# Hybrid decoder step on one core: pieces of the weights placed by the feature rows that they meet, units on feature rows eight apart, cache rows copied in pieces

## The chip, the cores and the metric

The kernel runs on one core of a Trainium2 chip. The metric is the device time of one execution in microseconds; of several runs the median counts. A profiled execution of the kernel gives a page of summaries and a trace that can be asked for single instructions.

## The reference, cut to what matters

One layer of a decoder works on 256 prompt rows and 8 sample rows, which share all weights. `IN_DIM` is 13856 columns, `D_FF` is 5632.

```python
h = RMSNorm(x)
q, k, v, z, xbc, dt, qm, g = split(h @ w_in)            # 2048 x 13856
a = sliding_window_attention(q, k, v)                    # sample: over a cache of 128 rows
s = ssd(xbc, z, dt)                                      # chunked scan, 32 heads
m = cross_attention(qm, mem)                             # mem @ w_mem_kv (2048 x 2048) for the prompt
x = x + (sig(gA)*(a @ w_up_swa) + sig(gB)*(s @ w_up_ssd) + sig(gM)*(m @ w_up_mem)) @ w_out
x = x + (silu(h2 @ w_gate) * (h2 @ w_up)) @ w_down       # h2 = RMSNorm(x), 2048 x 5632 and back
# also returned: the new keys, values, states, and the sample caches moved on by one row
```

Everything is float32. The sample caches `s_swa_k`, `s_swa_v` hold 127 old rows and one new one per sample, so 127 rows of 1 KB are copied for each of 8 samples, for keys and for values.

## The kernel before, in words

**Features and weights.** Activations lie in SBUF with the feature on the partition: feature row k is a slice of 128 partitions x 264 columns (256 prompt, 8 sample) of float32. Eight rows make one tile of `half` (pool `ap`, ten buffers); `Feat` is two such tiles, 16 rows of 2048 features. A weight matrix is used in groups of 512 output columns. A group has 4 PSUM tiles (128 output features each) and goes through its input features in units of two rows k. One unit is one load of 2 x 128 x 512 weights (512 KB) into `raw`.

**The split.** To keep precision, each unit's weights are split (`do_split`, helper `split`, L181 and L182): ScalarE writes `hi`, rounded to float32r, and VectorE writes `lo`, the rest. Features are split in the same way (`hh`/`hl`, `h2h`/`h2l`, `fah`/`fal`, `aTh`/`aTl`, `mTh`/`mTl`, `sT`, `mg`). A product is then three matmuls: hi with the high features, hi with the low ones, lo with the high ones. So a unit is 4 pieces c x 2 rows k x 3 = 24 matmuls of 128x128 weights with 264 moving columns. The helper `mm` records all of them at L160; they are told apart by the PSUM tile's name: `pin` (input projection), `pus`, `pum`, `pua` (the three up projections), `pout`, `pg`, `pu` (gate and up of the feed-forward), `pdn` (down). The memory projection `pmem` is turned round: there the features (`memh`, `meml`, 128 columns) are loaded as weights and 512 columns of `hi` or `lo` move.

**Addresses.** A feature row is 264 x 4 = 1056 bytes a partition, which is 4 x 256 + 32: each next row begins 32 bytes further within 256, and after eight rows it comes round. A piece of weights is 128 x 4 = 512 bytes, a whole multiple of 256. In the built program all `hi` and `lo` buffers begin at 128 within 256, so every piece does. With *offset* the text means the start of a piece minus the start of the feature row that moves with it, within 256 bytes. Before, it takes the eight values 0, 32, ..., 224, depending on the row alone. (The tile of `h2h` begins at 192 within 256, that of `hh` at 64: for `h2h` row 12 has offset 64 and row 13 has 32.)

**Order of the work.** A list `units` holds all units. The loop at the end of the kernel walks it: `feed` loads four units ahead and splits three ahead, then the unit's matmuls follow, then `after` of a group (which reads the PSUM tiles), then a slice of the side work (`side`, `slow`: attention, SSD, norms), whose pieces are told by estimated microseconds. A scheduler then places the recorded instructions, so that two units can be mixed in some places. Weight loads are issued on SP's queue, most other transfers on POOL's. `behind_split(d)` makes a DMA wait for the split last issued. `move_rows` copies the cache rows from DRAM to DRAM, in two DMAs of 1 MB and a small one for the convolution, and is called when the last group of `pout` begins.

```python
for k in range(2):
    kk = 2 * u + k
    wh = hi[:, k * 512 + c * P:k * 512 + (c + 1) * P]
    wl = lo[:, k * 512 + c * P:k * 512 + (c + 1) * P]
```

Of the kernel before, what the change touches and what calls it, by code (L numbers as in the profile page):

```python
# [18 lines left out]
P = 128  # L19
D = 2048  # L20
NP = 256
# [56 lines left out]
def tile_hybrid_decoder_step(  # L78
# [198 lines left out]
    def do_split(n):  # L277
        if n < state["split"]:
            return
        raw = raws.pop(n)  # L280
        hi = wp.tile([P, 1024], F32R, tag="hi", name=nm("hi"), bufs=3)
        lo = wp.tile([P, 1024], F32R, tag="lo", name=nm("lo"), bufs=3)
        if units[n].get("whole"):
            act(hi.bitcast(F32)[:, 0:512], raw[:, 0:512], AF.Copy)
        elif units[n].get("perm"):
            for k in range(2):
                v = [t[:, k * 512:(k + 1) * 512].rearrange("p (r a d) -> p a r d", r=4, a=2) for t in (hi, lo)]
                s = raw[:, k * 512:(k + 1) * 512].rearrange("p (a r d) -> p a r d", a=2, r=4)
                state["split_at"], state["rest_at"] = split(v[0], v[1], s)
        else:  # L290
            for k in range(2 if n == 0 else 1):
                c = slice(512 * k, 512 * k + 512) if n == 0 else slice(0, 1024)
                with tc.issue_after(state["memh", k if n == 0 else 1].ins):
                    state["split_at"], state["rest_at"] = split(hi[:, c], lo[:, c], raw[:, c])
        parts[n] = (hi, lo)
        state["split"] = n + 1

    def std_loads(src):
# [3 lines left out]

    def group(name, loads, nk, xh, xl, after, perm=False, before=None, middle=None):

        st = {}

        def prod(u):
            def f(hi, lo):
                if u == 0:
                    if before:  # L310
                        before()
                    st["ps"] = [dps(name)[:, 0:NT] for _ in range(4)]
                if middle and 2 * u == nk // 2:
                    middle()
                for c in range(4):
                    for k in range(2):
                        kk = 2 * u + k
                        wh = hi[:, k * 512 + c * P:k * 512 + (c + 1) * P]
                        wl = lo[:, k * 512 + c * P:k * 512 + (c + 1) * P]
                        mm(st["ps"][c], wh, xh(kk), start=kk == 0, stop=False)  # L320
                        mm(st["ps"][c], wh, xl(kk), start=False, stop=False)
                        mm(st["ps"][c], wl, xh(kk), start=False, stop=kk == nk - 1)
            return f

        for u in range(nk // 2):
            units.append(dict(
                loads=loads(u), perm=perm, prod=prod(u),
                after=(lambda: after(st["ps"])) if u == nk // 2 - 1 else None))

    def w_loads(w, col):  # L330
        return lambda u: std_loads(w[2 * u * P:(2 * u + 2) * P, col:col + 512])

# [37 lines left out]
    def mem_group(cg):  # L370
        st = {}

        def prod(u):
            def f(hi, lo):
                if u == 0:
                    st["ps"] = [dps("pmem") for _ in range(2)]
                for n, (t, k) in enumerate(((0, 0), (1, 0), (0, 1), (1, 1))):
                    if cg == 0 and n == 1 and u < 7:

                        with tc.issue_after(m.ins):  # L380
                            mem_feats(u + 1)
                    kk = 2 * u + k
                    mh = memh(kk)[:, t * P:(t + 1) * P]
                    ml = meml(kk)[:, t * P:(t + 1) * P]
                    wh, wl = hi[:, k * 512:(k + 1) * 512], lo[:, k * 512:(k + 1) * 512]
# [51 lines left out]
        for u in range(KT // 2):  # L437
            units.append(dict(
                loads=loads(u), 
                prod=prod(u), after=(after_k if cg < 2 else after_v) if u == KT // 2 - 1 else None))  # L440
# [74 lines left out]
    nd = const([P, 256], "nd")  # L515
    slope = const([P, 16], "slope")
    nslope = const([P, 16], "nslope")
    islope = const([P, 16], "islope")
    sink = const([P, 16], "sink")
    nsink = const([P, 16], "nsink")  # L520
    cols = const([P, 4], "cols")
    slope_c, islope_c, sink_c = cols[:, 0:1], cols[:, 1:2], cols[:, 2:3]
    blk2 = const([P, 62], "blk2")
    jm = const([32, 16], "jm")
    kn_bc = const([P, 64], "kn_bc")
    dtb_bc = const([P, 32], "dtb_bc")
# [70 lines left out]

    def move_rows():

        for dst, src in ((s_swa_k, cache_swa_k), (s_swa_v, cache_swa_v)):  # L600
            to, of = (t[0].rearrange("b t h d -> b (t h d)")[:, o:o + 127 * 256].rearrange("b (s e) -> s b e", s=16)
                      for t, o in ((dst, 0), (src, 256)))
            tc.keep_in_program_order(nc.gpsimd.dma_start(to, of))
        nc.gpsimd.dma_start(s_conv[0, :, 0:2], state_conv[0, :, 1:3])


# [225 lines left out]

    kT = const([P, 2, NT], "kT")

    v_new = const([P, 2, NS], "v_new")

# [260 lines left out]
    dt_tok = const([P, 64], "dt_tok")  # L1097
    last = const([P, 11, 24], "last")
    acs_tok = const([P, 64], "acs_tok")
# [8 lines left out]
    def conv(ct, raw, dst):  # L1108
# [10 lines left out]
        V.tensor_tensor(acc[:, :, NP:NT], acc[:, :, NP:NT], pre[:, ct:ct + 4], op=ALU.add)  # L1119
        act(dst, acc, AF.Silu)  # L1120
        V.tensor_copy(last[:, :, ct:ct + 4].rearrange("p r c -> p c r"), raw[:, :, NP - 3:NT])
        if ct == 12:
# [21 lines left out]

    def task_b():
        ssd["B"] = const([P, 4, NT], "BT")
        yield from conv(16, ssd["Braw"], ssd["B"])
# [40 lines left out]
    def task_dt():  # L1188
        ssd["dsc"] = const([P, 16, 17], "dsc", tag="nd")
        s3 = const([P, 3, 16, NS], "s3", tag="kT")  # L1190
        ssd["xsS"], ssd["zsS"], ssd["ysS"] = (s3[:, i] for i in range(3))
# [159 lines left out]
    def ssd_norm_work(g):  # L1351
        ssd[f"s{g}"] = half("sT", F32R)
        y, z = ssd[f"y{g}"][:, :, 0:NP], ssd[f"z{g}"]
# [27 lines left out]
        yield None  # L1381
        hi, lo = ssd[f"s{g}"][:, 0:4, 0:NP], ssd[f"s{g}"][:, 4:8, 0:NP]
        act(hi, y, AF.Copy)
# [25 lines left out]
    def ssd_sample_end():  # L1409
# [18 lines left out]
        for g in range(4):  # L1428
            split(ssd[f"s{g}"][:, 0:4, NP:NT], ssd[f"s{g}"][:, 4:8, NP:NT], t[:, 4 * g:4 * g + 4])
        yield 3  # L1430
# [107 lines left out]
    def up_mem(i):  # L1538
        branch("pum", C_G + 4096 + 512 * i, w_loads(w_up_mem[0], 512 * i),
               lambda k: mT["h"][:, k], lambda k: mT["l"][:, k].bitcast(F32R), mg_d[:, i],  # L1540
               middle=split_m if i == 0 else None)
# [42 lines left out]
    def after_ups(i):  # L1584
        def f(ps):
            mg[i] = half("mg", F32R)
            for c in range(4):
                tm = t1("mgs")
                V.tensor_tensor(tm, ps[c], mg["s", i][:, c], op=ALU.mult)
                V.tensor_tensor(tm, tm, mg["w", i][:, c], op=ALU.add)  # L1590
                split(mg[i][:, c], mg[i][:, 4 + c], tm)
        return f

    for i in range(4):
        group("pus", w_loads(w_up_ssd[0], 512 * i), KT, lambda k: ssd[f"s{k // 4}"][:, k % 4],
              lambda k: ssd[f"s{k // 4}"][:, 4 + k % 4], after_ups(i), before=lambda i=i: before_ups(i),
              middle=lambda i=i: middle_ups(i))

# [8 lines left out]
    def after_out(i):  # L1607
        def f(ps):
            if i == 0:
                x2["x"] = Feat("x2", F32)  # L1610
                x2["h"], x2["l"] = Feat("h2h"), Feat("h2l")
                x2["s"] = const([P, NT], "sqsum", tag="kT")
            for c in range(4):
# [22 lines left out]
    def before_out(i):  # L1636
        load_x(i)
        if i == 3:
            move_rows()

    for i in range(4):
        group("pout", w_loads(w_out[0], 512 * i), KT, lambda k: mg[k // 4][:, k % 4], lambda k: mg[k // 4][:, 4 + k % 4], after_out(i),
              before=lambda i=i: before_out(i))
# [28 lines left out]
    def down(i, base, nt_, last):  # L1672
# [32 lines left out]

        def loads(u):
            r = (4 * base + 2 * u) * P
            return std_loads(w_down[0, r:r + 2 * P, 512 * i:512 * (i + 1)])

        group("pdn", loads, nt_, lambda k: ffn["h"](k), lambda k: ffn["l"](k), after)  # L1710

    for base, ng in ((0, 4), (4, 4), (8, 3)):
# [33 lines left out]
    for i, u in enumerate(units):  # L1746
# [52 lines left out]
```

## Time and profile before

| what | value |
|---|---|
| median of 3 runs | 1902.41 us (1901.97 to 1904.27) |
| span of the profiled execution, first to last instruction | 1901.3 us |
| time of that execution beside its span | not listed apart; the runs shown lie 0.7 to 3.0 us above the span |
| TensorE busy | 1893.6 us, 100% of the span |
| VectorE, ScalarE, GpSimd busy | 1176.5, 959.8, 114.9 us |
| bytes moved | 402.08 MB, mean 211 GB/s |

Matmuls are pipelined: a row of the trace gives a matmul's start and a duration of some 285 ns, while the next one starts some 120 ns later. So the cost of a matmul is read from the distance between starts, or from the time of a whole stretch divided by its count, never from the mean duration. Rows of the timeline are rounded to 10 ns; a distance between two single rows is good to 10 ns, one over nine rows to about 1 ns each.

### The profile page before, as it was taken

The page shows a single profiled execution, that of the slowest core. Times are in us where ns is not written, and L with a number is a line of the kernel's source. Part 1 is how long each engine was busy: PE and PEld are TensorE (multiplying, and loading weights), DVE is VectorE, ACT ScalarE, POOL GpSimd, SP SyncE. Part 2 cuts the span into 40 slices and gives each one's busy share as a digit, 9 for nine tenths or more (in the row PEclk, how much of TensorE's full clock was granted, in tenths as well). Part 3 has the DMA queues.
Part 4 walks back from the last instruction along what each step waited for, and adds up shares of the span by engine and source line. Part 5 has one row for each costly group of instructions (what it writes and reads, how often), then busy time and mean ns, then how long its engine had stood idle before and what let it go on. Part 6 is the DMA issues. An engine that isn't in the chain of part 4 may idle for free.

```text
span 1901.3 us, 37640 instructions
## 1 busy us (share of the span) xinstructions
PE 1893.6 (100%) x15359; PEld 1848.2 (97%) x15359; DVE 1176.5 (62%) x2263; ACT 959.8 (50%) x1403; POOL 114.9 (6%) x237
## 2 busy tenths in 40 slices
PE   9999999999999999999999999999999999999999
PEld 7899999989999999999999999999999999999999
DVE  5755578666787868787455665555445555445554
ACT  6654466655767676764443444444334444334443
POOL 1110001011011111110000000000000000000000
PEclk9999999999999999999999999999999999999999
DMA  8776679678777777797768556665566665566654
GB/s 303 234 235 201 203 229 298 199 226 256 215 220 250 238 243 234 234 265 223 220 226 291 191 178 178 179 185 180 178 180 183 180 179 182 182 178 178 179 191 131
DMA packets 196898, 402.08 MB, mean 211 GB/s; under 512 B 16462, under 2 KB 22052, under 8 KB 196716
## 3 DMA queue, kind: packets, MB, share of 16 engines
q1 hardware_dynamic: 171856, 324.54, 56.1%
q0 software_dynamic: 19456, 69.08, 11.0%
q10 hardware_dynamic: 5412, 6.05, 0.9%
q8 instruction: 120, 1.97, 0.4%
q14 instruction: 54, 0.44, 0.1%
HBM read 375.71 MB, written 26.19 MB: 211 GB/s over the span
## 4 chain that ended last, share of the span: by engine, by line
PE 99%; DMA 1%; ACT 0%; issue 0%; SPq 0%; ACTq 0%
PE pin L160 33%; PE pu L160 14%; PE pdn L160 14%; PE pg L160 14%; PE pus L160 5%; PE pout L160 5%; PE pmem L160 4%; PE pum L160 2%; PE pua L160 2%; DMA raw<-in_w_mem_kv_dram 1%; PE py L160 1%; PE oms L160 0%; PE ps L160 0%; PE pst L160 0%; PE scm L160 0%; PE om L160 0%
## 5 line engine op out<-in xcount | busy, mean ns | idle before, releaser
L182 DVE TENSOR_TENSOR lo<-raw,hi 128x1024 fp32r<-128x1024 f32 (+1 forms) x625 | 744.9, 1194 | 586.3 <-ACT hi L181 582.3
L181 ACT ACTIVATE hi<-raw 128x1024 fp32r<-128x1024 f32 (+1 forms) x625 | 645.4, 1036 | 849.5 <-PE pin L160 203.6
L160 PE MATMUL pin<-hl,hi 128*128 128x264 f32 x1728 | 490.5, 286 | 0.0
L160 PE MATMUL pin<-hh,hi 128*128 128x264 f32 x1728 | 489.5, 286 | 0.0
L160 PE MATMUL pin<-hh,lo 128*128 128x264 f32 x1728 | 483.0, 286 | 0.0
L160 PEld LDWEIGHTS pin<-hh,hi 128*128 128x128 f32 x1728 | 325.4, 189 | 4.6 <-issue 4.2
L160 PEld LDWEIGHTS pin<-hl,hi 128*128 128x128 f32 x1728 | 325.2, 188 | 4.2 <-issue 4.0
L160 PEld LDWEIGHTS pin<-hh,lo 128*128 128x128 f32 x1728 | 320.7, 188 | 2.0 <-issue 1.6
L160 PE MATMUL pdn<-fah,hi 128*128 128x264 f32 x704 | 199.7, 285 | 0.0
L160 PE MATMUL pdn<-fal,hi 128*128 128x264 f32 x704 | 199.4, 285 | 0.0
L160 PE MATMUL pu<-h2h,hi 128*128 128x264 f32 x704 | 199.4, 284 | 0.0
L160 PE MATMUL pu<-h2l,hi 128*128 128x264 f32 x704 | 199.3, 284 | 0.0
L160 PE MATMUL pg<-h2l,hi 128*128 128x264 f32 x704 | 199.1, 285 | 0.0
L160 PE MATMUL pg<-h2h,hi 128*128 128x264 f32 x704 | 198.4, 284 | 0.0
L160 PE MATMUL pdn<-fah,lo 128*128 128x264 f32 x704 | 197.0, 284 | 0.0
L160 PE MATMUL pu<-h2h,lo 128*128 128x264 f32 x704 | 196.6, 284 | 0.0
L160 PE MATMUL pg<-h2h,lo 128*128 128x264 f32 x704 | 196.1, 284 | 0.0
L160 PEld LDWEIGHTS pu<-h2h,hi 128*128 128x128 f32 x704 | 132.8, 189 | 0.0
L160 PEld LDWEIGHTS pdn<-fah,hi 128*128 128x128 f32 x704 | 132.7, 189 | 0.0
L160 PEld LDWEIGHTS pg<-h2h,hi 128*128 128x128 f32 x704 | 132.7, 188 | 0.0
L160 PEld LDWEIGHTS pu<-h2l,hi 128*128 128x128 f32 x704 | 132.6, 188 | 0.0
L160 PEld LDWEIGHTS pdn<-fal,hi 128*128 128x128 f32 x704 | 132.6, 188 | 0.0
(520 smaller groups left out, 2923.1 us busy)
## 6 DMA issues: line engine op xcount, KB each, us to landing
raw<-in_w_in_dram SPq DMA_DIRECT2D x216, 512.0 KB
raw<-in_w_gate_dram SPq DMA_DIRECT2D x88, 512.0 KB
raw<-in_w_up_dram SPq DMA_DIRECT2D x88, 512.0 KB
raw<-in_w_down_dram SPq DMA_DIRECT2D x88, 512.0 KB
raw<-in_w_up_ssd_dram SPq DMA_DIRECT2D x32, 512.0 KB
raw<-in_w_out_dram SPq DMA_DIRECT2D x32, 512.0 KB
raw<-in_w_mem_kv_dram SPq DMA_DIRECT2D x31, 512.0 KB
ring<-in_state_ssm_dram POOLq DMA_DIRECT2D x32, 256.0 KB, 4.9
```

The source lines that it names most:

```text
L160: return nc.tensor.matmul(out, lhsT=lhsT, rhs=rhs, start=start, stop=stop)
L181: h = act(hi, src, AF.Copy)
L182: return h, V.tensor_tensor(lo, src, hi.bitcast(F32), op=ALU.subtract)
```

## The change

It has four parts.

1. `do_split` writes the two halves of a unit to places (`places`) that depend on the feature rows they will meet. The buffers `hi` and `lo` grow from 1024 to 1088 columns. Each half is put 32 columns plus 8 columns for each row within eight behind the buffer's start (modulo 64 columns, 256 bytes). In the built program the offset, as defined above, is then 32 in every main matmul; for `pmem`, where it is the stationary features minus the moving weights, it is 32 too. The weights that are being loaded for the next matmul have offset 32 to the row that is moving in nearly all cases; at the change of unit it is 64, 0 or another value for one matmul.
2. `couples`: a unit takes rows u and u + 8 in place of 2u and 2u + 1 (where there are 16), so that both rows of a unit begin at the same place within 256. For the groups of 8 rows the pairs stay neighbours, for the 12 rows of the last `pdn` they are (4,5), (6,7), (0,8), (1,9), (2,10), (3,11). `w_loads` reads the matching weight rows. `sT` and `mg` now keep high and low parts in separate tiles, so both parts of a row begin at the same place too.
3. The cache rows are copied in 16 pieces of 127 KB and one for the convolution, one piece after each unit of the feed-forward from the second on, each behind a split. `middle_ups` (the load of a gate tile) runs at the second unit of an ups group, not at the middle one.
4. To make room in SBUF, small constants share one tile `pack` with `last`, and `kT`, `Btok`, `s3`, `sqsum` share tiles in another way.

```diff
-        hi = wp.tile([P, 1024], F32R, tag="hi", name=nm("hi"), bufs=3)
-        lo = wp.tile([P, 1024], F32R, tag="lo", name=nm("lo"), bufs=3)
+        hi = wp.tile([P, 1088], F32R, tag="hi", name=nm("hi"), bufs=3)
+        lo = wp.tile([P, 1088], F32R, tag="lo", name=nm("lo"), bufs=3)
+        at = units[n].get("at")
...
+            step = at[1] - at[0]
+            if n == 0 or at[0] + 2 * step > 1088:
+                halves = [(slice(512 * k, 512 * k + 512), *(t[:, at[k]:at[k] + 512] for t in (hi, lo))) for k in range(2)]
+            elif step == 512:
+                halves = [(slice(0, 1024), *(t[:, at[0]:at[0] + 1024] for t in (hi, lo)))]
+            else:
+                halves = [(slice(0, 1024), *(t[:, at[0]:at[0] + 2 * step].rearrange("p (k n) -> p k n", k=2)[:, :, 0:512]
+                                             for t in (hi, lo)))]
...
+    OFFSET = 32
+    def places(rows, first=OFFSET):
+        a, b = ((8 * (r % 8) + first) % 64 for r in rows)
+        return a, 512 + b + (64 if b < a else 0)
+    def couples(nk):
+        if nk == 8:
+            return [(2 * u, 2 * u + 1) for u in range(4)]
+        if nk == 12:
+            return [(4, 5), (6, 7), (0, 8), (1, 9), (2, 10), (3, 11)]
+        return [(u, u + nk // 2) for u in range(nk // 2)]
...
-                    for k in range(2):
-                        kk = 2 * u + k
-                        wh = hi[:, k * 512 + c * P:k * 512 + (c + 1) * P]
-                        wl = lo[:, k * 512 + c * P:k * 512 + (c + 1) * P]
-                        mm(st["ps"][c], wh, xh(kk), start=kk == 0, stop=False)
+                    for k, kk in enumerate(couples(nk)[u]):
+                        n = 2 * u + k
+                        wh, wl = (t[:, at[u][k] + c * P:at[u][k] + (c + 1) * P] for t in (hi, lo))
+                        mm(st["ps"][c], wh, xh(kk), start=n == 0, stop=False)
...
-    def w_loads(w, col):
-        return lambda u: std_loads(w[2 * u * P:(2 * u + 2) * P, col:col + 512])
+    def w_loads(w, col, nk=KT, first=0):
+        rows = w.rearrange("(k p) n -> p k n", p=P)
+        def f(u):
+            a, b = (first + k for k in couples(nk)[u])
+            return lambda raw: [(raw.rearrange("p (k n) -> p k n", k=2), rows[:, a:b + 1:b - a, col:col + 512])]
+        return f
...
-            tc.keep_in_program_order(nc.gpsimd.dma_start(to, of))
+        if i > ffn["first"] and moves:
+            behind_split(nc.gpsimd.dma_start(*moves.pop()))
```

What stands on TensorE's queue in the first unit of a gate group (`pg`), before; the two tiles `h2h_1731`, `h2l_1733` hold rows 0 to 7:

```order
L160 MATMUL pg_1844_13771<-h2h_1731_12906,hi_1825_13634 128x264
L160 MATMUL pg_1844_13771<-h2l_1733_12908,hi_1825_13634 128x264
L160 MATMUL pg_1844_13771<-h2h_1731_12906,lo_1826_13635 128x264
L160 MATMUL pg_1844_13771<-h2h_1731_12906,hi_1825_13634 128x264
L160 MATMUL pg_1844_13771<-h2l_1733_12908,hi_1825_13634 128x264
L160 MATMUL pg_1844_13771<-h2h_1731_12906,lo_1826_13635 128x264
```

The first three use row 0, the next three row 1, 32 bytes further. The same place on TensorE's queue after the change (`h2h_1732`, `h2l_1734` hold rows 8 to 15):

```order
L160 MATMUL pg_1844_13760<-h2h_1731_12898,hi_1825_13623 128x264
L160 MATMUL pg_1844_13760<-h2l_1733_12900,hi_1825_13623 128x264
L160 MATMUL pg_1844_13760<-h2h_1731_12898,lo_1826_13624 128x264
L160 MATMUL pg_1844_13760<-h2h_1732_12899,hi_1825_13623 128x264
L160 MATMUL pg_1844_13760<-h2l_1734_12901,hi_1825_13623 128x264
L160 MATMUL pg_1844_13760<-h2h_1732_12899,lo_1826_13624 128x264
```

The second three now use row 8, which begins at the same place within 256 as row 0; the number and kind of matmuls is as before. The end of POOL's queue before, from the last gate tiles of the ups groups on:

```order
L1604 DMA xT_12664<-xT_d 128x1056
L1604 DMA xT_12939<-xT_d 128x1056
L1604 DMA xT_13209<-xT_d 128x1056
L1582 DMA sgi_12521<-sg_d 128x1056
L1604 DMA xT_13479<-xT_d 128x1056
L603 DMA out_dram<-in_cache_swa_k_dram 16x8x2032
L603 DMA out_dram<-in_cache_swa_v_dram 16x8x2032
```

And the same end of POOL's queue after it:

```order
L1637 DMA xT_12656<-xT_d 128x1056
L1637 DMA xT_12931<-xT_d 128x1056
L1637 DMA xT_13201<-xT_d 128x1056
L1613 DMA sgi_12424<-sg_d 128x1056
L1637 DMA xT_13471<-xT_d 128x1056
L1793 DMA out_dram<-in_state_conv_dram 8x6144
L1793 DMA out_dram<-in_cache_swa_v_dram 16x2032 x8
L1793 DMA out_dram<-in_cache_swa_k_dram 16x2032 x8
```

Two large copies became sixteen small ones, and the one for the convolution rows, which stood further ahead before, came to them; nothing of the program is queued behind them.

More of the change, by code (lines that the diff above doesn't have):

```diff
@@ L290, in do_split @@
         else:
-            for k in range(2 if n == 0 else 1):
-                c = slice(512 * k, 512 * k + 512) if n == 0 else slice(0, 1024)
+            step = at[1] - at[0]
[6 more added lines that the diff above has]
+                                             for t in (hi, lo)))]
+            for k, (c, h, l) in enumerate(halves):
+                src = raw[:, c] if len(h.shape) == 2 else raw.rearrange("p (k n) -> p k n", k=2)
                 with tc.issue_after(state["memh", k if n == 0 else 1].ins):
-                    state["split_at"], state["rest_at"] = split(hi[:, c], lo[:, c], raw[:, c])
+                    state["split_at"], state["rest_at"] = split(h, l, src)
         parts[n] = (hi, lo)
         state["split"] = n + 1
+    OFFSET = 32
[8 more added lines that the diff above has]
+        return [(u, u + nk // 2) for u in range(nk // 2)]
     def std_loads(src):
@@ L301, in std_loads, with group @@
         return f
-    def group(name, loads, nk, xh, xl, after, perm=False, before=None, middle=None):
+    def group(name, loads, nk, xh, xl, after, perm=False, before=None, middle=None, early=None):
         st = {}
+        at = [places(rows) for rows in couples(nk)]
         def prod(u):
@@ L371, in mem_group @@
         st = {}
+        at = [places((2 * u, 2 * u + 1), OFFSET - 16) for u in range(KT // 2)]
         def prod(u):
@@ L384, in f @@
                     ml = meml(kk)[:, t * P:(t + 1) * P]
-                    wh, wl = hi[:, k * 512:(k + 1) * 512], lo[:, k * 512:(k + 1) * 512]
+                    wh, wl = (t[:, at[u][k]:at[u][k] + 512] for t in (hi, lo))
                     mm(st["ps"][t], mh, wh, start=kk == 0, stop=False)
@@ L438, in mem_group @@
             units.append(dict(
-                loads=loads(u),
+                loads=loads(u), at=at[u],
                 prod=prod(u), after=(after_k if cg < 2 else after_v) if u == KT // 2 - 1 else None))
@@ L515, in tile_hybrid_decoder_step @@
     nd = const([P, 256], "nd")
[L516 to L521, printed above, removed]
+    pack = const([P, 11 * 24], "pack", tag="last")
+    slope, nslope, islope, sink, nsink = (pack[:, 128 + 16 * i:144 + 16 * i] for i in range(5))
+    cols = pack[:, 208:212]
     slope_c, islope_c, sink_c = cols[:, 0:1], cols[:, 1:2], cols[:, 2:3]
-    blk2 = const([P, 62], "blk2")
+    blk2 = pack[:, 0:62]
     jm = const([32, 16], "jm")
-    kn_bc = const([P, 64], "kn_bc")
+    kn_bc = pack[:, 64:128]
     dtb_bc = const([P, 32], "dtb_bc")
@@ L596, in consts @@
             yield 1
[L598 to L604, printed above, removed]
+    moves = []
+    for dst, src in ((s_swa_k, cache_swa_k), (s_swa_v, cache_swa_v)):
+        for b in range(NS):
+            moves.append([t[0, b].rearrange("t h d -> (t h d)")[o:o + 127 * 256].rearrange("(s e) -> s e", s=16)
+                          for t, o in ((dst, 0), (src, 256))])
+    moves.append((s_conv[0, :, 0:2], state_conv[0, :, 1:3]))
     def h_group(col, after, perm=False, before=None, middle=None):
@@ L1120, in conv @@
         act(dst, acc, AF.Silu)
+        last = ssd["last"]
         V.tensor_copy(last[:, :, ct:ct + 4].rearrange("p r c -> p c r"), raw[:, :, NP - 3:NT])
@@ L1145, in task_b @@
     def task_b():
+        ssd["last"] = const([P, 11, 24], "last")
         ssd["B"] = const([P, 4, NT], "BT")
@@ L1351, in ssd_norm_work @@
     def ssd_norm_work(g):
-        ssd[f"s{g}"] = half("sT", F32R)
+        if g % 2 == 0:
+            for s in "hl":
+                ssd[f"s{s}{g // 2}"] = half("sT", F32R)
         y, z = ssd[f"y{g}"][:, :, 0:NP], ssd[f"z{g}"]
@@ L1381, in ssd_norm_work @@
         yield None
-        hi, lo = ssd[f"s{g}"][:, 0:4, 0:NP], ssd[f"s{g}"][:, 4:8, 0:NP]
+        hi, lo = (ssd[f"s{s}{g // 2}"][:, 4 * (g % 2):4 * (g % 2) + 4, 0:NP] for s in "hl")
         act(hi, y, AF.Copy)
@@ L1428, in ssd_sample_end @@
         for g in range(4):
-            split(ssd[f"s{g}"][:, 0:4, NP:NT], ssd[f"s{g}"][:, 4:8, NP:NT], t[:, 4 * g:4 * g + 4])
+            hi, lo = (ssd[f"s{s}{g // 2}"][:, 4 * (g % 2):4 * (g % 2) + 4, NP:NT] for s in "hl")
+            split(hi, lo, t[:, 4 * g:4 * g + 4])
         yield 3
@@ L1585, in f @@
         def f(ps):
-            mg[i] = half("mg", F32R)
+            if i % 2 == 0:
+                for s in "hl":
+                    mg[s, i // 2] = half("mg", F32R)
             for c in range(4):
@@ L1590, in f @@
                 V.tensor_tensor(tm, tm, mg["w", i][:, c], op=ALU.add)
-                split(mg[i][:, c], mg[i][:, 4 + c], tm)
+                split(*(mg[s, i // 2][:, 4 * (i % 2) + c] for s in "hl"), tm)
         return f
     for i in range(4):
-        group("pus", w_loads(w_up_ssd[0], 512 * i), KT, lambda k: ssd[f"s{k // 4}"][:, k % 4],
-              lambda k: ssd[f"s{k // 4}"][:, 4 + k % 4], after_ups(i), before=lambda i=i: before_ups(i),
-              middle=lambda i=i: middle_ups(i))
+        group("pus", w_loads(w_up_ssd[0], 512 * i), KT, lambda k: ssd[f"sh{k // 8}"][:, k % 8],
+              lambda k: ssd[f"sl{k // 8}"][:, k % 8], after_ups(i), before=lambda i=i: before_ups(i),
+              early=lambda i=i: middle_ups(i))
     x2 = {}
@@ L1637, in before_out @@
         load_x(i)
-        if i == 3:
-            move_rows()
     for i in range(4):
-        group("pout", w_loads(w_out[0], 512 * i), KT, lambda k: mg[k // 4][:, k % 4], lambda k: mg[k // 4][:, 4 + k % 4], after_out(i),
+        group("pout", w_loads(w_out[0], 512 * i), KT, lambda k: mg["h", k // 8][:, k % 8], lambda k: mg["l", k // 8][:, k % 8], after_out(i),
               before=lambda i=i: before_out(i))
@@ L1704, in after @@
                         (nc.scalar if f else nc.sync).dma_start(y_sample.rearrange("b s d -> (b s) d")[:, cols_], ot[P - NS:P])
[L1706 to L1710, printed above, removed]
+        group("pdn", w_loads(w_down[0], 512 * i, nt_, 4 * base), nt_, lambda k: ffn["h"](k), lambda k: ffn["l"](k), after)
+    ffn["first"] = len(units)
     for base, ng in ((0, 4), (4, 4), (8, 3)):
```

19 lines of the change are left out of this document (10 added, 9 removed).

## The prediction

> **What bounds the kernel now.** I read the page's first two parts, then the chain that ended last, and then the timeline of TensorE alone, since the first two leave nothing else. The page:
>
> ```profile
> PE 1893.6 (100%) x15359; PEld 1848.2 (97%) x15359; DVE 1176.5 (62%) x2263; ACT 959.8 (50%) x1403; POOL 114.9 (6%) x237
> PEclk9999999999999999999999999999999999999999
> PE 99%; DMA 1%; ACT 0%; issue 0%; SPq 0%; ACTq 0%
> raw<-in_w_in_dram SPq DMA_DIRECT2D x216, 512.0 KB
> raw<-in_w_gate_dram SPq DMA_DIRECT2D x88, 512.0 KB
> raw<-in_w_up_dram SPq DMA_DIRECT2D x88, 512.0 KB
> raw<-in_w_down_dram SPq DMA_DIRECT2D x88, 512.0 KB
> raw<-in_w_up_ssd_dram SPq DMA_DIRECT2D x32, 512.0 KB
> raw<-in_w_out_dram SPq DMA_DIRECT2D x32, 512.0 KB
> ...
> raw<-in_w_up_mem_dram SPq DMA_DIRECT2D x16, 512.0 KB
> raw<-in_w_up_swa_dram SPq DMA_DIRECT2D x32, 256.0 KB
> ```
>
> TensorE works all the time at its full granted clock and makes 99% of the chain; VectorE and ScalarE, which split the weights, are at 62% and 50%. So only the time of a matmul counts. The load rows give the number of main matmuls: 216 + 3 x 88 + 2 x 32 + 16 + 16 (of two halves each) = 576 units, times 24 is 13,824. The chain gives the time of each:
>
> ```profile
> 932.16 94.11 PE pus L160 x768
> 1026.27 94.03 PE pout L160 x768
> 1144.05 23.39 PE pu L160 x192
> 1167.44 23.35 PE pg L160 x192
> 1307.66 93.53 PE pdn L160 x768
> ```
>
> The second column is the stretch's time: 23.35 / 192 = 121.6 ns for `pg`, 121.8 for `pu` and `pdn`, 122.5 for `pus`, 122.4 for `pout`. The last two are those whose high and low features stood four rows (128 bytes) apart. I take 121.7 ns as the mean over all: 13,824 x 121.7 ns = 1682 us, 88% of the 1901.3 us span.
>
> How fast could it be? The nearest row without any such delay is `scm`, plain float32 with 256 columns:
>
> ```profile
> 171.77 1.89 PE L160 MATMUL scm<-kmT,qmT 128*128 128x256 f32 x8
> L160 PE MATMUL scm<-kmT,qmT 128*128 128x256 f32 x32 | 7.6, 379 | 0.0
> ```
>
> Eight of them take 1.89 us and the last one's own time is 379 ns, so the starts lie (1.89 - 0.379) / 7 = 216 ns apart. Read as two columns in the time that the float32r matmuls have for four, that is an estimated 216 / 2 x 264 / 256 = 111 ns for 264 columns at full rate. The main matmuls are some 10 ns above it, and the change can only work on these 10 ns.
>
> By the Trainium skill ("TensorE: Matmul & The Clock Gate", Back-to-back issue gap) a warm matmul takes N / 2.4 + 2.5 ns, 112.5 ns here; the 121.7 ns of the trace are above that as well.
>
> **Does the offset set the 10 ns?** The trace of before holds all eight offsets, so I looked for places where one offset lasts. Mostly it holds for three matmuls (one row k). The scheduler mixed units in a few places, which gives longer runs. The first row of each pair below opens a run of equal offset in `pin`, the second follows its last matmul (offset 0, nine matmuls; offset 128, eight; offset 64, nine):
>
> ```profile
> 679.14 0.28 PE L160 MATMUL pin<-hh,hi 128*128 128x264 f32 x1
> 680.21 0.28 PE L160 MATMUL pin<-hh,hi 128*128 128x264 f32 x1
> 713.31 0.28 PE L160 MATMUL pin<-hl,hi 128*128 128x264 f32 x1
> 714.27 0.28 PE L160 MATMUL pin<-hh,hi 128*128 128x264 f32 x1
> 716.10 0.28 PE L160 MATMUL pin<-hh,hi 128*128 128x264 f32 x1
> 717.21 0.29 PE L160 MATMUL pin<-hh,hi 128*128 128x264 f32 x1
> ```
>
> They give 1.07 / 9 = 119 ns, 0.96 / 8 = 120 ns, 1.11 / 9 = 123 ns. So equal offsets do not bring 111 ns; they bring 119 to 123. Offset 32 occurs only in threes. In `pg`, with rows 12 (offset 64) and 13 (offset 32):
>
> ```profile
> 1418.96 0.29 PE L160 MATMUL pg<-h2h,hi 128*128 128x264 f32 x1
> 1419.09 0.28 PE L160 MATMUL pg<-h2l,hi 128*128 128x264 f32 x1
> 1419.20 0.28 PE L160 MATMUL pg<-h2h,lo 128*128 128x264 f32 x1
> 1419.33 0.28 PE L160 MATMUL pg<-h2h,hi 128*128 128x264 f32 x1
> ...
> 1419.69 0.29 PE L160 MATMUL pg<-h2h,hi 128*128 128x264 f32 x1
> 1419.81 0.28 PE L160 MATMUL pg<-h2l,hi 128*128 128x264 f32 x1
> 1419.93 0.28 PE L160 MATMUL pg<-h2h,lo 128*128 128x264 f32 x1
> 1420.06 0.28 PE L160 MATMUL pg<-h2h,hi 128*128 128x264 f32 x1
> ```
>
> Rows 1, 2 and 3 of each half have offset 32; the fourth is the next piece, at 64. A three takes 0.37 us with the step from 64 to 32 in it, 123 ns a matmul. From the second on it is (1419.33 - 1419.09) / 2 and (1420.06 - 1419.81) / 2, 120 to 125 ns at this rounding.
>
> The second witness is `pmem`, where six matmuls in a row have one offset and the next ones load during 512 columns:
>
> ```profile
> 101.29 0.39 PE L160 MATMUL pmem<-hi,memh 128*128 128x512 f32 x1
> ...
> 103.38 0.40 PE L160 MATMUL pmem<-hi,memh 128*128 128x512 f32 x1
> ```
>
> Nine starts in 2.09 us are 232 ns. At the full rate estimated above it would be 216, so the delay is 16 ns on 512 columns against 10 on 264. It grows with the columns that move, though one load of weights falls to each matmul in both. That speaks for a delay that mostly belongs to the moving row itself, and against one that a better offset to the weights removes.
>
> **The change part by part.**
>
> *Offsets and pairs.* The steps of offset inside a unit go, and a constant 32 stays. I take 120.8 ns: between the runs' 119, 120 and 123, nearest to the settled ones, and at the lower end of what the threes at 32 show after their first matmul. Sum: 13,824 x (121.7 - 120.8) = 12.4 us less. Bounds: 119 gives 37 us less, 123 gives 18 us more. In `pus` and `pout` the high and low parts now agree too; that is in the mean. The 384 `pmem` stay at 232 ns: 0, at most 384 x 16 = 6 us less.
>
> *Splits.* As many instructions, each on 1024 columns, to places a few columns further; where the pair's rows are neighbours the output has two pieces. Even a tenth more on both engines would lie under VectorE's 38% of free time: 0.
>
> *Loads.* The same 512 KB on SP's queue, from two blocks of 128 rows that lie further apart, no instruction more: 0, hidden while four loads run ahead.
>
> *Which row is needed when.* Row 8 and up are now needed from the first unit. This moves the last features of a group from the fifth or seventh unit to the third or fifth. The tightest place is the last `pdn`:
>
> ```profile
> 1821.99 18.25 PE pdn L160 x150
> L182 DVE TENSOR_TENSOR fal<-us,fah x4: 426/427/427, 1824.9 to 1825.9; 128x264 fp32r<-128x264 f32 x4
> ```
>
> The last low parts are done at 1825.9 + 0.4 = 1826.3, 4.3 us after the group begins. Before they were needed after four units, 4 x 24 x 0.1217 = 11.7 us; now after two, 5.8 us. The pairs (4,5), (6,7) keep 1.5 us of cover: 0. If it is gone, the wait is one of at most 4 us.
>
> *Cache copies.* On POOL the two issues cost half a microsecond each, and nothing waits behind them:
>
> ```profile
> 1030.23 0.56 POOL L603 DMA_DIRECT2D out_dram<-in_cache_swa_k_dram  x1
> 1030.79 0.55 POOL L603 DMA_DIRECT2D out_dram<-in_cache_swa_v_dram  x1
> ```
>
> `pout` ran through them at 122.4 ns, like `pus` before (122.5). Seventeen pieces wait for a split each, alone on a queue with nothing behind. 0. The earlier gate tile (`middle_ups`) and the shared small tiles: 0, no engine but TensorE is near its limit, and the owners' work stands in order in the side list.
>
> Sum: 1901.3 - 12.4 = 1888.9 us of span. The median stands 1.1 us above the span: 1890.0 us.
>
> **Rivals.** *The collisions go.* If the 10 ns come from weights and features that meet in the same place of SBUF, and offset 32 in a long steady stream avoids it, a matmul takes between the 111 ns of `scm` and 118: 13,824 x 10.7 = 148 us less at most, 51 us at 118, so 1754 to 1851 us. For it: time does move with the offset (119 against 123). Against it: none of the steady runs comes near, and `pmem` loses more with longer rows.
>
> *No effect.* The delay is the moving row's own and the steps of offset cancel: 1902 us, within 3.8 us. For it: `pmem`, and that `pg` and `pdn` agree within 0.2 ns whatever their rows. The Trainium skill says so outright ("SBUF — State Buffer", Who interferes with whom): TensorE has two independent read ports, one for the moving operand and one for the weights, and never waits on anyone. The runs at 119 and 123 ns do not fit it wholly.
>
> *Slower.* Offset 32 is a bad one. Place: every main matmul; price: the threes' 123 ns, 13,824 x 1.3 = 18 us more, 1920 us. It decides as soon as the settled time at 32 is above 121.7 ns. For it: the first matmul at 32 is slow wherever 64 goes before, and offset 64 in its run is the slow one. Against it: what comes after the first is at the mean or below.
>
> *The offsets are not met.* They hang on where the buffers begin; in the built program they hold, so only the one matmul at a change of unit differs. No chance of its own.
>
> **How the numbers follow.** My forecast (faster, 1870 to 1898.6) has 0.42; the collisions go (below 1870) 0.24; no effect 0.15; slower 0.19. The measurement tells 0.2%, 3.8 us, from no change. So faster 0.66, same 0.15, slower 0.19. The likeliest case's own range is 1870 to 1899. The range for 8 in 10, 1825 to 1912, adds no effect, somewhat under half of the first rival and over half of the slower one: 0.42 + 0.15 + 0.11 + 0.11 = 0.79.
>
> **What would show it.** In the chain, `pg` x192 at 23.2 us (23.35 now) shows my size, below 22.7 the first rival, 23.35 no effect, 23.6 the slower one. `pus` and `pout` should fall to the others' time. `pmem` should stay at 232 ns. TensorE's waits should stay below a few microseconds; a wait at the third unit of the last `pdn` shows that cover gone. I am wrong above all if long streams at one offset settle elsewhere than runs of nine.

## The result, and the profile after

The changed kernel took 1882.84 us (median; 1881.55 to 1884.94), the one before 1903.32 us beside it: ratio 0.989, 95% interval 0.988 to 0.991. The profiled execution has a span of 1881.0 us against 1901.3. The page of the changed kernel, its engines and the granted clock:

```profile
PE 1873.3 (100%) x15359; PEld 1827.8 (97%) x15359; DVE 1175.1 (62%) x2263; ACT 959.9 (51%) x1403; POOL 121.6 (6%) x251
PEclk9999999999999999999999999999999999999999
```

TensorE still works all the time at the same clock; it does the same 15,359 instructions in 20.3 us less. The chain of the changed kernel (start, duration, what, count) shows where:

```profile
925.42 92.24 PE pus L160 x768
1017.66 92.48 PE pout L160 x768
1133.66 23.06 PE pu L160 x192
1156.72 23.06 PE pg L160 x192
1295.08 92.24 PE pdn L160 x768
1802.40 18.07 PE pdn L160 x150
```

23.06 / 192 = 120.1 ns a matmul in `pg` and `pu` (121.6 and 121.8 before), 92.24 / 768 = 120.1 in `pdn` and `pus` (121.8, 122.5), 120.4 in `pout` (122.4). Adding all distances from the start of a main matmul to the next start, by family: `pin` -5.7 us, `pu` -3.7, `pg` -3.2, `pdn` -3.3, `pus` -1.9, `pout` -1.5, `pum` and `pua` -0.3, together 19.5 us of the 20.3. Of the rest, 0.6 us is a shorter wait at `memT`. TensorE's list of waits is still short:

```profile
PE idle L160 <- DVE warm L213: 1.5, 1, 1.5
PE oms L160 <- DMA ld<-in_cache_mem_v_dram: 0.7, 1, 0.7
PE memT L164 <- DMA mem<-in_mem_prompt_dram: 0.5, 1, 0.5
```

In the tightest place, the last `pdn`, the low features are written here:

```profile
L182 DVE TENSOR_TENSOR fal<-us,fah x4: 429/429/431, 1805.3 to 1806.3; 128x264 fp32r<-128x264 f32 x4
```

They are done at 1806.3 + 0.4 = 1806.7 us; two units after the group's start are 1802.40 + 48 x 0.12 = 1808.2. The group's 150 matmuls run through at 18.07 / 150 = 120.5 ns.

So in `pg`, `pu`, `pdn`, `pout` and `pus` a matmul became 1.5 to 2.4 ns shorter, in `pin` 1.1 ns, in `pum` and `pua` 0.5 and 0.3 ns. Three questions were open: whether the pairs, the constant offset or its value does it; why it stops at 120.1; and whether the other parts of the change count.

### The profile page after: what moved, and what is told of

The parts are those of the page before. It is cut to its first block, busy times and chain, and to the rows that moved or that the text cites. A ratio compares the mean times of both kernels' runs of the same rounds, so it can differ in the third digit from the quotient of the medians.

```text
span 1881.0 us, 37669 instructions
## 1 busy us (share of the span) xinstructions
PE 1873.3 (100%) x15359; PEld 1827.8 (97%) x15359; DVE 1175.1 (62%) x2263; ACT 959.9 (51%) x1403; POOL 121.6 (6%) x251
## 4 chain that ended last, share of the span: by engine, by line
PE 77%; issue 2%; DMA 0%; POOL 0%; DVE 0%; ACT 0%; ACTq 0%; POOLq 0%
PE pin L160 19%; PE pdn L160 13%; PE pg L160 13%; PE pu L160 13%; PE pout L160 5%; PE pus L160 5%; PE pum L160 2%; PE pua L160 2%; PE py L160 1%; PE pst L160 0%; DMA ld<-in_cache_mem_v_dram 0%; PE yt L164 0%; PE xtok L164 0%; PE oms L160 0%; PE cb L160 0%
## 5 line engine op out<-in xcount | busy, mean ns | idle before, releaser
L160 PEld LDWEIGHTS pg<-h2l,hi 128*128 128x128 f32 x704 | 132.0, 187 | 0.0
```

What stands on the lines that cost most here:

```text
L160: return nc.tensor.matmul(out, lhsT=lhsT, rhs=rhs, start=start, stop=stop)
```

## Experiment 1: matmuls alone

> A kernel of matmuls alone: it leaves the whole decoder step out, loads one block of weights, and runs sections of 96 matmuls that differ in offset, columns or data type, first with no other engine at work, then again with ScalarE, VectorE and DMA busy. Theory 'steps' (a change of offset costs, a constant one does not, whatever its value): all constant offsets within 1 ns of each other, at 120 ns for 264 columns; only the two sections with alternating offsets are slower, by 1 to 3 ns. Theory 'value' (32 is a good offset, others are bad): the constant sections differ by 2 ns or more, and 32 is among the best, 64 or 224 among the worst. Theory 'traffic' (the remaining 8 ns over 112 come from other engines' reads and writes): quiet sections at 111 to 113 ns, the same sections with traffic at 120. Theory 'per column' (the rest belongs to the moving row): the interval over the columns stays near 0.454 ns a column for 264 to 512 columns, quiet or not.

```python
a, b = wo // 4 + 128 * c + 576 * k, xo // 4 + 576 * k     # wo: the section's offset, bytes
w, x = (wl if j == 2 else wh)[:, a:a + 128], (xl if j == 1 else xh)[:, b:b + n]
nc.tensor.matmul(ps[c][:, 0:n], lhsT=w, rhs=x, ...)
```

The timeline of TensorE, first matmul of a section and first of the next: offset 32 and offset 160 without other work, then offsets 32 and 160 (192 matmuls each) with other work, and the table of windows for the last two (DMA share and GB/s at the end):

```profile
52.36 0.28 PE L90 MATMUL p<-xh,wh 128*128 128x264 f32 x1
63.88 0.28 PE L90 MATMUL p<-xh,wh 128*128 128x264 f32 x1
145.37 0.29 PE L90 MATMUL p<-xh,wh 128*128 128x264 f32 x1
157.53 0.28 PE L90 MATMUL p<-xh,wh 128*128 128x264 f32 x1
598.96 0.28 PE L90 MATMUL p<-xh,wl 128*128 128x264 f32 x1
622.00 0.29 PE L90 MATMUL p<-xh,wl 128*128 128x264 f32 x1
692.11 0.28 PE L90 MATMUL p<-xh,wl 128*128 128x264 f32 x1
715.47 0.28 PE L90 MATMUL p<-xh,wl 128*128 128x264 f32 x1
```

```profile
598.96:622.00 23.04, 23.04 (x195) 23.04 (x193) 23.04 (x21) 20.74 (x21) 0.00 (x0) 1.00 0.81 237
692.11:715.47 23.36, 23.36 (x194) 23.36 (x193) 23.36 (x21) 21.09 (x20) 0.00 (x0) 1.00 0.80 239
```

Offset 32: 11.52 / 96 = 120.0 ns in quiet and 23.04 / 192 = 120.0 with VectorE full and 237 GB/s of transfers. So at offset 32 the traffic costs nothing, and "traffic" falls. Offset 160: 126.7 quiet, 121.7 later. Each kernel of matmuls alone was profiled once. The means of all quiet sections (after the first twelve matmuls, ns):

| offset | 0 | 16 | 32 | 48 | 64 | 80 | 96 | 112 | 128 | 144 | 160 | 176 | 192 | 208 | 224 | 240 |
|---|---|---|---|---|---|---|---|---|---|---|---|---|---|---|---|---|
| ns | 120.0 | 120.0 | 120.0 | 120.0 | 120.0 | 120.0 | 121.7 | 124.4 | 120.0 | 122.6 | 126.7 | 120.0 | 121.0 | 121.7 | 122.3 | 120.0 |

With the offset held at 32, moving the feature row itself to seven other places within 256 bytes left it at 120.0 each time: at this offset only the difference of the two addresses counts. The value does matter, so "steps" as I had it falls, and 32 is among the best; but 64, which theory 'value' had among the worst, is as good, and no value gives less than 120.0. Of the sections with mixed offsets, 32 with 0 stayed at 120.0, 32 with 128 took 122.1. With traffic, offset 128 took 123.3 and 160 took 121.7: some offsets have more than one pattern in which they settle.

## Experiment 2: the change in halves

`order` keeps offset 32 but reads neighbours; `pairs` reads rows eight apart but puts the weights where they were:

```diff
 # order, in couples (the two special cases for nk go as well)
-        return [(u, u + nk // 2) for u in range(nk // 2)]
+        return [(2 * u, 2 * u + 1) for u in range(nk // 2)]
 # pairs, in places
-        return a, 512 + b + (64 if b < a else 0)
+        return 0, 512
```

> The changed kernel with its features in the old order (units read neighbours), the offset 32 kept for every matmul. If the constant offset is the cause, it stays with the changed kernel: 0.989 of before, pg at 120.2 ns. If the pairing matters by itself, it goes back towards before: 0.993 to 1.0.

> The changed kernel with its pairs eight apart, but all weights at fixed places, so that the offset is constant within a unit and steps by 32 from unit to unit (about 1,000 steps instead of 5,700). Theory 'steps': 1013 of 5689 steps are left, so about 0.82 of the gain is kept, 0.991 of before. Theory 'value': the mean over eight offsets, as before, 0.997 to 1.0.

`order` took 1890.88 us, ratio 0.993 (0.992 to 0.994); `pairs` 1903.64 us, 1.000 (0.999 to 1.001). The chains, `order` first, then `pairs`:

```profile
1160.86 23.20 PE pg L160 x192
```

```profile
1167.60 23.39 PE pg L160 x192
```

120.8 and 121.8 ns. A constant offset inside each unit, without its value, is worth nothing; my "steps" predicted 0.991 for it. And the pairs matter although a matmul's own offset is 32 in both kernels: without them about a third of the gain is lost. What differs between `order` and the changed kernel is the *next* matmul's weights: when k goes from a row to its neighbour, the weights loaded meanwhile lie 32 bytes further from the row still moving (offset 64, or 0 on the way back). Rows eight apart begin at the same place within 256 bytes, so there the load in flight has offset 32 too. That is a guess that the next run tests.

## Experiment 3: which weights meet the row

> Matmuls alone again (the rest of the step is left out), 264 columns unless said: the row patterns of before (neighbours, fixed weights), of 'pairs' (rows eight apart, fixed weights), of 'order' (neighbours, weights at +32) and of the changed kernel (rows eight apart, +32), 192 matmuls each; two-place patterns in which a matmul's own weights have one offset and the next ones, which load while it runs, another; 512 columns at 16 offsets; and offsets entered from other offsets. Theory 'next weights' (what collides is the load of the next weights with the row that moves): before and pairs near 121.5 to 122.5, order 120.5 to 121.5, changed 120.0; own 32 with next 160 slow (above 124), own 160 with next 32 at 120.0. Theory 'own weights': the reverse for the last two, and order equal to changed. 512 columns: 226.7 at offset 0 and 233.3 at 32, as in the first such run. If an offset settles in the same way from wherever it is entered, the entries change nothing; if not, 128, 160 and 0 take two values each, and 32 and 64 one.

```python
# turn: own offset p1 for every matmul, moving row p2 bytes further in every second one
b = 576 * k + p2 // 4 * (i % 2); a = 576 * k + 128 * c + (p1 + p2 * (i % 2)) // 4
# rows: feature row r = (u, u + 8)[k] or (2 * u, 2 * u + 1)[k], 264 columns each
```

The timeline; each row begins a section, in the order: before, pairs, order, changed (192 matmuls each), own offset 32 with the next at 160, own 160 with the next at 32 (96 each), and the section after:

```profile
33.13 0.28 PE L79 MATMUL p<-xh,wh 128*128 128x264 f32 x1
56.47 0.28 PE L79 MATMUL p<-xh,wh 128*128 128x264 f32 x1
79.78 0.29 PE L79 MATMUL p<-xh,wh 128*128 128x264 f32 x1
102.94 0.29 PE L79 MATMUL p<-xh,wh 128*128 128x264 f32 x1
125.99 0.29 PE L79 MATMUL p<-xh,wh 128*128 128x264 f32 x1
137.82 0.28 PE L79 MATMUL p<-xh,wh 128*128 128x264 f32 x1
149.34 0.28 PE L79 MATMUL p<-xh,wh 128*128 128x264 f32 x1
```

23.34 / 192 = 121.6, 121.4, 120.6 and 120.05 ns for the four row patterns: the full kernels' order, with nothing but TensorE at work. The last two decide it: own 32 with next 160 takes 11.83 / 96 = 123.2 ns, own 160 with next 32 takes 120.0. So in these two sections the cost follows the offset between the row that moves and the weights of the neighbouring matmul, not a matmul's own pair. It was below the 124 ns that I expected. That it is the *next* matmul's weights, and not the ones before, rests on the trace: the load of the next weights (PEld) starts with the matmul, as below with the first one of own 32, while the load of the ones before, 0.19 us long from a start 0.24 us earlier, is over.

```profile
125.99 0.19 PEld L79 LDWEIGHTS p<-xl,wh 128*128 128x128 f32 x1
```

One thing does not follow from these offsets. In the pattern of `order` the load in flight meets only 32, 64 and 0, and each of the three, held in quiet, took 120.0 in the first run, as did 32 and 0 by turns of three. Yet the pattern takes 120.6. So steps between good offsets can cost as well; why, no run here shows. The two sections meant for 96 had it in every second matmul only (224 or 160 in the others) and decide nothing.

The entries, by the second half of each section: 32 and 64 settled at 120.0 from every start; 0 at 121.4 after 160 and at 120.0 after the others; 128 at 123.3 after 0 and 64 and at 120.0 after 32, 160 and 192; 160 at 120.0 after 64 and at 121.6 after the others, while the first run had it at 126.7.

With 512 columns, offsets 0, 16 and 240 gave 226.7 ns, 32 gave 233.3, the others 229 to 234.

## Experiment 4: other offsets in the full kernel

One number is changed, `OFFSET`, to 56, 0 and 40 columns (offsets 128, 160 and 64).

> The changed kernel with offset 128 in place of 32, constant for every matmul. Theory 'steps': the same as the changed kernel, 0.989 of before within 0.001. Theory 'value': slower than it, above 0.993, or faster if 32 is not the best.

> The changed kernel with offset 160 for every main matmul and for pmem, constant throughout. Theory 'value' from the quiet run alone: 126.7 against 120.0 ns, 13,824 x 6.7 = 92 us more than the changed kernel, 1975 us; if it settles as under traffic, 121.7 ns, 23 us more, 1906 us. Theory 'steps': the same as the changed kernel, 1883 us.

> The changed kernel with offset 64 in place of 32. Any offset that settles at 120.0 ns in the matmuls alone should do: within 3 us of the changed kernel run beside it, a little above if the step to 96 at a change of unit (121.7 ns) tells. If 32 is a value of its own: 5 us or more slower.

> The changed kernel again, beside off64 on the same chip: 0.989 of before.

| offset | us | ratio to before, interval |
|---|---|---|
| 32 (again) | 1883.19 | 0.990 (0.988 to 0.991) |
| 128 | 1886.42 | 0.991 (0.990 to 0.993) |
| 64 | 1895.17 | 0.996 (0.994 to 0.997) |
| 160 | 1917.10 | 1.007 (1.006 to 1.009) |

A constant offset can thus make the kernel slower than before. Two expectations were missed: 128 lies between the two that I wrote down (0.989 and above 0.993), and 160 lies between my two sums, 11 us above the lower one. `pg` in the chains of 128, 64 and 160:

```profile
1160.04 23.07 PE pg L160 x192
```

```profile
1162.41 23.23 PE pg L160 x192
```

```profile
1174.12 23.57 PE pg L160 x192
```

120.2, 121.0 and 122.8 ns. Offset 64 missed my expectation too: 12.0 us above the changed kernel beside it, not at most 3, though alone it settles at 120.0 like 32. In its trace the first matmuls of a unit take 127 to 132 ns before it is back at exactly 120. The last kernel asked whether the step to the next unit's row does that, or the interruptions by other matmuls.

> Matmuls alone, the rest of the step left out: units as in the changed kernel (24 matmuls on two rows eight apart, the next unit one row on, 264 columns) at 16 constant offsets, eight units each, first without a break, then with one small plain-float32 matmul in every second unit. In the full kernels pg took 120.1 ns at offset 32, 120.1 at 128, 121.1 at 64 and 122.8 at 160. Theory 'step to the next unit' (what off64 lost is the one load in 24 that meets a row at offset 96): the sections without a break show it, 64 about 1 ns above 32. Theory 'breaks' (64 recovers slowly after an interruption): 64 equals 32 at 120.0 without a break and lies above it with one. Neither: 64 equals 32 in both, and the cause stays in the full kernel.

```python
r = (u, u + 8)[k]                                        # unit u, as in the changed kernel
a, b = 128 * c + 576 * k + (8 * r + d // 4) % 64, r * NT  # constant offset d
```

The timeline at the first matmul of a section (192 matmuls each). The first two rows are offsets 0 and 16; then in pairs offsets 32, 64, 128 and 160, each followed by the first of the next section:

```profile
32.00 0.28 PE L70 MATMUL p<-xh,wh 128*128 128x264 f32 x1
55.27 0.28 PE L70 MATMUL p<-xh,wh 128*128 128x264 f32 x1
78.42 0.29 PE L70 MATMUL p<-xh,wh 128*128 128x264 f32 x1
101.47 0.28 PE L70 MATMUL p<-xh,wh 128*128 128x264 f32 x1
124.55 0.29 PE L70 MATMUL p<-xh,wh 128*128 128x264 f32 x1
147.78 0.29 PE L70 MATMUL p<-xh,wh 128*128 128x264 f32 x1
217.61 0.28 PE L70 MATMUL p<-xh,wh 128*128 128x264 f32 x1
240.66 0.29 PE L70 MATMUL p<-xh,wh 128*128 128x264 f32 x1
264.21 0.28 PE L70 MATMUL p<-xh,wh 128*128 128x264 f32 x1
287.82 0.28 PE L70 MATMUL p<-xh,wh 128*128 128x264 f32 x1
```

Offsets 32, 64, 128 and 160 take 120.05, 121.0, 120.05 and 123.0 ns, against 120.1, 121.0, 120.2 and 122.8 in the full kernels. The step to the next unit does it: held without steps, 64 took 120.0. A unit at 64 took 2897 to 2905 ns after the first one, one at 32 took 2879 to 2881, so the step costs some 20 ns; 576 units in the full kernel make that 12 us, an estimate, and 64 lost 12.0.

Why the step costs 64 so much is not shown. At the step the next unit's first weights come 32 bytes higher while the old row still moves, offset 96 for a kernel at 64, and 96 is slow when held (121.7). But this does not hold in general: at 176 the step meets 208, as slow as 96 when held, and costs nothing (120.1 ns), and so does 128, where it meets 160 (120.0 to 126.7 when held, by what ran before); at 0 and 16 it meets 32 and 48, both good when held, and yet 0 takes (55.27 - 32.00) / 192 = 121.2 ns and 16 takes 120.6. So neither the values held nor the values met at the step tell which offset is good in units; it has to be measured with its steps.

The half with breaks says nothing of 64: the small matmuls did not run where they were written; two thirds of them stood ahead of the first section and the rest in the last five sections, offsets 160 to 240.

`pg` is equal at 128 and 32, and yet 128 is 3 us slower. The difference arises in the `pin` stage (`pus` begins at 928.76 us instead of 925.42), and there after a break: in the first three dozen `pin` matmuls behind another matmul the distances average 129.7, 122.0 and 121.3 ns by dozens at 128, and 128.1, 120.7 and 120.4 at 32; from the fourth dozen on the two agree within 0.2 ns. That is some 2.9 us of the 3.8 that `pin` takes longer.

## Experiment 5: what the 120 ns are

> Matmuls alone, the rest of the step left out: 264 columns of float32r with 32, 64, 96 or 128 columns of weights at offsets 32, 96, 160 and 224; bfloat16 with 264 columns at eight offsets; 256 and 384 columns of float32r at eight offsets. Theory 'reads collide' (what is above 112.5 ns is time in which the weights' load and the moving row read the same part of SBUF): fewer weights' columns bring the 120.0 ns down towards 112.5 (about 114 for 32 columns) and shrink the spread over the offsets; bfloat16, which reads half the bytes on both sides, stays at 112.5 at every offset. Theory 'float32r streams at 0.4545 ns a column': 120.0 whatever the weights' columns, and 174.5 for 384.

The timeline: offset 32 with 32 weight columns begins in the first row and ends at the second; offset 160 with 32 columns in the third and fourth; then the first of 768 bfloat16 matmuls (eight offsets) and the first after them; then 96 float32r matmuls of 384 columns and the first after:

```profile
28.23 0.28 PE L73 MATMUL p<-xh,wh 128*32 128x264 f32 x1
39.75 0.28 PE L73 MATMUL p<-xh,wh 128*32 128x264 f32 x1
51.48 0.28 PE L73 MATMUL p<-xh,wh 128*32 128x264 f32 x1
63.30 0.28 PE L73 MATMUL p<-xh,wh 128*32 128x264 f32 x1
214.71 0.40 PE L73 MATMUL p<-bx,bw 128*128 128x264 bf16 x2
301.04 0.36 PE L73 MATMUL p<-xh,wh 128*128 128x256 f32 x1
392.22 0.34 PE L73 MATMUL p<-xh,wh 128*128 128x384 f32 x1
408.86 0.34 PE L73 MATMUL p<-xh,wh 128*128 128x384 f32 x1
```

A quarter of the weights leaves 11.52 / 96 = 120.0 ns at offset 32, and 123.1 at 160: the floor is not the bytes of the weights. bfloat16 takes 86.33 / 768 = 112.4 ns, and 112.5 in each of its eight sections, whatever the offset. So both things, the 120 instead of 112.5 and the dependence on the offset, belong to float32r here. 384 columns take 173.3 ns at the offset shown, 0: bfloat16's 112.5 scaled to 384 columns is 163.6, so the excess is 9.7 ns, against 7.5 at 264 columns. "Reads collide" in its simple form (fewer bytes, less delay) falls as to the floor, though the spread over the four offsets did shrink, from 6.5 ns with 128 columns of weights to 3.1 with 32; "0.4545 ns a column" holds at 264 columns, while 384 took 173.3 to 176.7 by the offset. How many columns are loaded or move changes the good offsets: with 64 columns of weights, 32 took 123.4 and 160 took 120.0; with 256 moving columns, 96 took 117.3, and 0, 128 and 160 took 120.0. What makes the floor stays open.

## Experiment 6: pmem and the cache copies

```diff
 # pmem0
-        at = [places((2 * u, 2 * u + 1), OFFSET - 16) for u in range(KT // 2)]
+        at = [places((2 * u, 2 * u + 1), OFFSET - 8) for u in range(KT // 2)]
 # oldmoves
+        if i == 3:
+            move_rows()          # in before_out: two DMAs of 1 MB, as before
-        if i > ffn["first"] and moves:
-            behind_split(nc.gpsimd.dma_start(*moves.pop()))
```

> The changed kernel with offset 0 in place of 32 for the 384 pmem matmuls alone. From the 512-column sections of the run of matmuls alone, 226.7 against 233.3 ns: 384 x 6.6 = 2.5 us less than the changed kernel, 1880.3 us. If pmem's delay does not hang on the offset: the same as the changed kernel.

`pmem0` took 1882.01 us, 0.989 (0.987 to 0.990), no more than the scatter away from the changed kernel. Undisturbed `pmem` matmuls went from a mean of 232.3 to 230.4 ns, 384 x 1.9 = 0.7 us, not 2.5: no six matmuls in a row reached the 226.7 held alone. In the kernel the rows and places step every six matmuls, which may be why.

> The changed kernel with the cache rows copied by two large transfers and one small, where before had them, in the last quarter of pout. If the pieces bring nothing (the prediction's term of 0): the same as the changed kernel within 2 us, 0.989 of before. If the two large transfers held something up: 4 us or more above it.

`oldmoves` took 1886.12 us, 0.991 (0.989 to 0.993), 4.1 us above `pmem0` on the same chip; the intervals overlap. Its trace has a candidate for part of it. In time the copies run near the start of `pout`, at 1022.6 us, as they did before. The list of TensorE's waits and the chain there:

```profile
PE pout L160 <- ACT hi L181: 1.1, 1, 1.1
PE pout L160 <- DVE lo L182: 0.8, 1, 0.8
```

```profile
1022.98 12.19 DMA raw<-in_w_out_dram
```

The same two views of `pmem0`, which has the pieces:

```profile
PE pout L160 <- DVE lo L182: 0.6, 1, 0.6
```

```profile
1001.80 13.38 DMA raw<-in_w_out_dram
```

In `oldmoves` a load of weights took 12.19 us beside the two copies, and the split behind it kept TensorE waiting. But a load of 13.38 us, with a wait of 0.6 us behind it, stands in `pmem0` too, 21 us earlier and with no copies beside it; so a slow load here is not the copies' doing alone. `pout` takes 94.7 us from its first start to the end of its last distance, against 93.2 in `pmem0` and 92.5 in the changed kernel. That the pieces save 1.5 to 2.2 us in this kernel is thus likely and not shown; the rest of the 4.1 us is not accounted for. Against before, no gain of the pieces is seen: in before the same copies lay beside `pout` with no wait, and `pairs`, which has the pieces, the shared tiles, the earlier gate tile and the new couples of rows but not the offsets, took 1.000 of before. So without the placement the other parts together gain nothing.

## Why the prediction came out as it did

Predicted 1890.0 us and faster; measured 1882.84, within the likeliest case's own range of 1870 to 1899. That the sign came out right was in part luck: the reason given, that the steps inside a unit go, holds as well for offsets 64 and 160, and these took 1895.17 and 1917.10 us. For 32 itself the rows of before showed only threes, at 120 to 125 ns by their rounding. Point by point:

- *The settled time of 120.8 ns* was the mis-sized term. It is 120.1 in `pg`, `pu` and `pus`: 13,824 x 0.7 = 9.7 us more gain than I took. `pin`, where other matmuls come between, gained 5.7 / 5184 = 1.1 ns instead of 1.6, about 2.6 us less; what `pus` and `pout` gained above 1.6 and `pum` and `pua` below it about cancel. 12.4 + 9.7 - 2.6 = 19.5, and 19.5 was measured. The 121.7 before was no mean over all either, as I had it: with the breaks in `pin` the mean distance was 122.6 ns before and is 121.2 now. The gain, 1.4 ns, not the level, carries the sum.
- *Its reason was only half right.* I held that the steps inside a unit go and that the settled time of a steady offset stays. `pairs`, with steady offsets inside a unit, gained nothing; so the value is needed. And `order`, with the value but with steps, gained two thirds; so the steps do cost something. I looked at the offset of a matmul's own weights in the trace of before, while own 32 with next 160 and the reverse tell that the neighbouring weights matter. The runs of nine that I called settled were not the settled time: the one at 64 read 123 ns and the one at 0 read 119, while alone both settle at 120.0 (0 at 121.4 from one start).
- *The collisions go* (1754 to 1851): wrong in its price. The 111 ns came from plain float32; float32r has its own floor, 120.0 ns at 264 columns, below which none of 16 offsets goes, nor a quarter of the weights.
- *No effect*: `pmem` was no witness for it, since 512 columns, held alone, took 226.7 to 234 ns by the offset. The other argument, independent reads, does not hold in the runs. The Trainium skill ("SBUF — State Buffer", Who interferes with whom) gives TensorE independent ports for moving rows and weights. Own 32 with next 160 took 123.2 ns and the reverse 120.0; for float32r the two are not independent here, and the measurement decides; for bfloat16, at 112.5 ns everywhere, it agrees. The section says nothing of offsets, and no run here shows in what part of the chip the two meet.
- *Slower*: offset 32 is not a bad one, but the rival was real for another constant: 160 makes the kernel slower than before.
- *pmem stays at 232*: 232.3. *`pus` and `pout` fall to the others' time*: 120.1 and 120.4. *`pg` at 23.2 us*: 23.06.
- *Cache copies 0*: right against before as far as `pairs` tells; in the changed kernel `oldmoves` leaves room for some 2 us, which is not shown. *The last pdn's cover of 1.5 us*: 1808.2 - 1806.7 = 1.5, and no wait.

## What to carry to other kernels

When TensorE is busy all the time, divide a stretch by its count and compare it with a run of the same matmuls alone at its best layout: 121.7 against 120.0 ns told here what could be had at most. For float32r, look at the address of the weights being loaded relative to the row that moves meanwhile, also across the step to the next row and the next unit. Measure the offsets alone, with the kernel's own steps and breaks, before building one in: held without steps, 64 and 0 are as good as 32, in units they are not; 160 cost 14 us where 32 brought 20; and the good values change with the number of columns.

## What the runs showed of the hardware

Float32r matmuls of 264 columns settle at a mean of 120.0 ns at the good offsets, bfloat16 at 112.5. The Trainium skill ("TensorE: Matmul & The Clock Gate", Back-to-back issue gap) gives N / 2.4 + 2.5 ns for an isolated warm matmul, 112.5 here: bfloat16 agrees, back to back, and float32r does not. The distances repeat in short patterns, at good offsets (122 and 118 ns by turns at 32) as at slow ones (127, 126, 127 at 160), and 0, 128 and 160 have more than one pattern, chosen by what ran before.

In the run of matmuls alone, a stretch of matmuls with 64 to 192 columns lost almost half its granted clock (0.57) though TensorE was never idle; the table of windows for it:

```profile
296.00:340.00 44.00, 44.00 (x236) 44.00 (x235) 0.00 (x0) 0.00 (x0) 0.00 (x0) 0.57 0.00 1
```

Starts lay 213 ns apart in its slow part and 110 to 113 before and after. What set it off stays open: 96 matmuls of 128 columns later in the same run (443 to 453 us) kept 1.00. The main matmuls here have 264 columns and kept 1.00 throughout.
